# One written order for the recurrence's preparation and its loop: fillers placed by each iteration's room, modulation parts apart

## The chip, the core and the metric

The kernel runs on one core of one Trainium2 chip. The core has a matrix engine (TensorE, PE in the profile; PEld are its weight loads), a vector engine (VectorE, DVE), an engine for activation functions (ScalarE, ACT), a general engine (GpSimd, POOL) and SyncE (SP), which here only issues DMA transfers. Each engine works through its own instructions in the order in which they stand; a semaphore makes one wait for another. The metric is the time of one execution in microseconds (us), lower is better; the figure given for a kernel is the median of its runs.

## The reference

One layer of a diffusion backbone over 256 latent and 256 context tokens, width 2048, in fp32. The parts that matter here:

```python
m_lat = jnp.split((silu(c) @ w_mod + b_mod), 6)            # modulation rows
h  = modulate(rmsnorm(x, norm1_g), m_lat[0], m_lat[1])
P  = h @ w_in                                              # dense projection
b_r = rwkv_branch(P)          # two directions, 16 heads, state carried over time
b_c = conformer_branch(P)     # ends in u @ w_conv_out
m  = (sigmoid(P_gate_r) * b_r + sigmoid(P_gate_c) * b_c) @ w_o
x  = x + m_lat[2] * m
x  = x + m_lat[5] * ec_moe(modulate(rmsnorm(x, norm2_g), m_lat[3], m_lat[4]))
out = rmsnorm(x, final_g)
```

The recurrence inside `rwkv_branch` is `S_t = S_{t-1} (diag(w_t) - kk_t^T (kk_t * a_t)) + v_t^T k_t`, `y_t = S_t r_t`. The modulation rows 2 to 5 are first needed after the recurrence, and so are the two gates of 2048 columns each.

## The kernel before

The program runs in stages: norms, the first modulation rows and the projections that feed the recurrence (to about 540 us), the recurrence with its preparation (540 to 1295 us), two output projections (to 1470 us), and sixteen experts, whose weights stream in (to the end).

**The recurrence.** There are 16 units, a pair of heads in one direction each (`units`, 8 pairs x 2). A unit is a Python generator, `rwkv_dir`, which is cut by `yield` into named steps: D0 to D6 (loads `km`, `kn`, `rm`, `lw`, `vm`; decay and gates by a small matmul with `lwh` and `lwl`, L664 and L665; scans; `KB` and `VK`), C0 to C5 (transposes L761, scores L750), A0 to A7 (inverse of a triangular block: L845, L852, L867, L877, L887) and B0 to Z6 and B2 (L893, then L914, which is the first matmul of the chain over time, then seven links L932 with an ACT copy `Z` in between, then the outputs L938 and L942). `run(i, last)` drives unit i until it yields `last`, so a step is the code ahead of its `yield`. Units of the second direction go on through the group norm, G0 to G3 (L982, L987, L993).

**The loop.** Iteration i runs the B steps of unit i, the A steps of unit i+1, the C steps of unit i+2 and the D steps of unit i+3. The table `PLAN` gives each step a number on a scale of 36 for one iteration; everything is sorted by that number and written out. Inside `tc.manual_schedule` PE and DVE keep the written order; ACT, POOL and SP are ordered by the scheduler from its own timeline.

**The fillers.** Between the steps stand pieces of dense work that the recurrence doesn't need. A *gate part* (`gate_part`) is half of a block of four 128x128 weights: six matmuls L234 to L236 on a bank `big`. Its weights come as `wraw` (DMA), are split into `whi` (ACT, L159) and `wlo` (POOL, L230), three buffers each. There are 320 parts; the last 16 are held back until after the loop, the first 12 are issued ahead of the preparation at low priority (`early`), and 292 are in the loop. A *modulation part* (`mod_steps`, `part`) is four matmuls of 512 columns (L284; two records each in the trace) on 1 MB of `w_mod`, which is loaded into `wm`. There is one `wm` buffer. Four parts make a row; after the fourth ACT copies the sum back into the `wm` buffer, and `finish` turns the row into a column (L301) and adds the bias on DVE. `finish` is put on the list `later` and runs when the next modulation part is due, that is, directly ahead of the first part of the next row. Eight rows are in the loop, one in every second iteration (the even ones).

`spread` gives each of the 16 iterations the same total weight of fillers (a gate part counts 0.5 and a modulation part 0.5), and the fillers of an iteration stand at even distances on the scale.

**The preparation.** Before the loop, unit 0 has to come through D, C and A, unit 1 through D and C, and unit 2 through D. These six calls of `run` stand ahead of `manual_schedule`, and the scheduler orders all engines there.

Of the kernel before, what the change touches and what calls it, by code (L numbers as in the profile page):

```python
# [32 lines left out]
HOLD = 2  # L33
# [33 lines left out]
MN = 4  # L67
# [4 lines left out]
REL = [[0], [2], [4]]  # L72
LOWP = 1500
F0, F1 = 0.5, 36.0
PLAN = [(0, 0, "B0"), (4.5, 0, "B1"), (6.5, 0, "Z0"), (8.5, 0, "Z1"), (10.5, 0, "Z2"), (12.5, 0, "Z3"), (14.5, 0, "Z4"), (16.5, 0, "Z5"), (18.5, 0, "Z6"),
# [4 lines left out]
MODS = [8]  # L80
# [61 lines left out]
def kernel(  # L142
# [450 lines left out]
    modf = [f for _, f in mids]  # L593

    def weave2(a, b):
        nc_ = 16 - MODS[0]
        m = len(b) // nc_ if nc_ else 1
        at = lambda i: (i // m + 0.1 + MSP * (i % m + 0.5) / m) / nc_
        t = sorted([((i + 0.5) / len(a), 0, i) for i in range(len(a))] + [(at(i), 1, i) for i in range(len(b))])
        return [(a, b)[n][i] for _, n, i in t]  # L600

    def spread(l):
        n, c, o = sum(w for w, _ in l), 0, [[] for _ in range(16)]
        for w, f in l:
            o[int((c + 0.5 * w) * 16 / n)].append(f)
            c += w
        return o

    fills = spread(weave2(gates, mids))
    pend, acc = [], [0.0, 1.0]  # L610

    def tick(c):
        if not PUMP:
            return
        acc[0] += c
        while pend and acc[0] >= acc[1]:
            acc[0] -= acc[1]
            flush(1)

    def flush(n):  # L620
        with tc.high_priority(offset=-LOWP):
            for f in pend[:n]:
                while later and f in modf:
                    later.pop(0)()
                f()
            del pend[:n]

    rw_stack = ExitStack()
    rw = rw_stack.enter_context(tc.tile_pool(name="rw", bufs=1))
    BUF = dict(VK=1, KB=1, a2=7, rm=2, bon=3, RB=3, WCk=3, t4=2, VU=3, KBt=3, t2=3, NT8=2, t1=5, tx=2, c2=3,   # L630
               ys=3, Pv=1, km=1, kn=1, gw=2, bonr=1, tmp=2)
# [8 lines left out]
    def rwkv_dir(p, d, bonr, bon, INP):  # L640
# [223 lines left out]
        for cp, h, c, q in each():  # L864
            a, b, i = 64 * q + e, 64 * q + o, 2 * cp + h
            tick(0.03)
            PE.matmul(pq[b:b + 32, i, 0:32], AT[a:a + 32, c, h, o:o + 32], T2[a:a + 32, i], start=True, stop=True)  # L867
# [6 lines left out]
        for cp, h, c, q in each():  # L874
            a, b, i = 64 * q + e, 64 * q + o, 2 * cp + h
            tick(0.03)
            PE.matmul(pq[a:a + 32, i, 0:32], Q[b:b + 32, i], TT[b:b + 32, i], start=True, stop=True)  # L877
# [7 lines left out]
        for cp, h, c, q in each():  # L885
            tick(0.07)
            mark["pv"] = PE.matmul(pv[hs(q), cp, h], AT[hs(1 - q), c, h], VU[hs(1 - q), c, h], start=True, stop=True)  # L887
# [142 lines left out]
    def fill(f):  # L1030
        while later and f in modf:
            later.pop(0)()
        f()
# [390 lines left out]
```

## Time and profile before

| what | time |
|---|---|
| runs shown | 2429.71 and 2433.34 us, median 2431.53 us |
| the profiled execution | 2426.3 us, its span 2424.5 us |
| last projection matmul of the stage ahead | ends at 540.4 us |
| L914 of unit 0 (the chain over time begins) | 612.3 us |
| L993 of the last unit (the last matmul of the recurrence) | ends at 1295.3 us |
| first matmul of the experts | 1480.4 us |

A *window* is below the time from one unit's first L914 to the next one's; it is an iteration's length as PE sees it, shifted a little against the scale (L914 stands at 4.5 of 36). A row of the windows view gives a stretch (start:end in us), its length, for each engine its busy time and number of records, then the granted PE clock (1.00 is full speed), the busy share of the DMA engines and GB/s. A row of the timeline gives start, duration, engine, line, operation, tiles, shapes and count, and in brackets the idle time ahead of it and what ended it.

### The profile page before, as it was taken

To read this page: it belongs to the slowest core of one execution; us is meant where nothing else is said; L and a number is where in the kernel's file an instruction comes from. 1 tells how busy PE (TensorE), PEld (TensorE's weight loads), DVE (VectorE), ACT (ScalarE), POOL (GpSimd) and SP (SyncE) were. 2 spreads that over 40 slices of the span, in tenths; PEclk is the share of its full clock that TensorE was granted. 3 is DMA by queue.
4 is the path that set the end of the run, shared out by engine and by line. 5 is a ranking of instruction groups with operands and counts; after the bars stand their busy time and mean duration, and the time that the engine had idled before them with its cause. 6 is when DMAs were issued, how large, how long until landed. Compare 5 with 4: busy or idle time off the path is not lost.

```text
span 2424.5 us, 49050 instructions
## 1 busy us (share of the span) xinstructions
PE 2002.5 (83%) x20778; PEld 1413.1 (58%) x20778; DVE 920.7 (38%) x1821; ACT 777.5 (32%) x1540; POOL 675.5 (28%) x706
## 2 busy tenths in 40 slices
PE   7999999995889789888978997877777777777765
PEld 3787888884768668667768994433333333333332
DVE  2348989425545445445322542212111111111112
ACT  3255344634556446446444551000000000000002
POOL 1343334335555456445435741000000000000002
PEclk9999999995989889889989998989888899898887
DMA  9958767662343443444345887999999999999995
GB/s 383 347 176 292 244 202 238 215 215 84 129 149 108 138 145 114 146 150 116 113 152 168 285 303 320 427 428 427 428 427 427 428 428 427 427 427 428 428 417 222
DMA packets 147228, 674.43 MB, mean 278 GB/s; under 512 B 17600, under 2 KB 38208, under 8 KB 109888
## 3 DMA queue, kind: packets, MB, share of 16 engines
q1 hardware_dynamic: 129488, 459.68, 52.2%
q10 hardware_dynamic: 17520, 211.61, 20.7%
q8 instruction: 163, 2.67, 0.5%
q14 instruction: 57, 0.47, 0.1%
HBM read 649.41 MB, written 21.82 MB: 277 GB/s over the span
## 4 chain that ended last, share of the span: by engine, by line
DMA 28%; PE 18%; ACT 2%; DVE 1%; issue 1%; POOL 1%; SPq 1%; ACTq 0%; DVEq 0%; POOLq 0%
DMA wx<-in_w_dn 17%; DMA wx<-in_w_gu 9%; PE rw L1266 3%; PE p L1335 2%; PE gn L1335 2%; PE rw L234 1%; PE rw L1295 1%; PE rw L236 1%; PE rw L235 1%; PE big L1303 1%; ACT ye L159 1%; DMA wm<-in_w_mod 1%; PE big L234 1%; PE big L235 0%; PE big L236 0%
## 5 line engine op out<-in xcount | busy, mean ns | idle before, releaser
L230 POOL TENSOR_TENSOR wlo<-wraw,whi 128x512 fp32r<-128x512 f32 x292 | 400.1, 1373 | 513.2 <-ACT whi L159 455.6
L1303 PE MATMUL big<-wx,xse 128*32 128x512 f32 x2048 | 299.7, 719 | 153.9 <-DMA wx<-in_w_gu 152.0
L159 ACT ACTIVATE whi<-wraw 128x512 fp32r<-128x512 f32 x428 | 264.0, 628 | 332.5 <-DMA wraw<-in_w_in 102.4
L234 PE MATMUL big<-hh,whi 128*128 128x256 f32 x912 | 282.3, 310 | 2.7 <-ACT whi L159 2.7
L1303 PEld LDWEIGHTS big<-wx,xse 128*32 128x32 f32 x2048 | 63.7, 122 | 356.0 <-issue 179.9
L1279 POOL TENSOR_TENSOR r<-r 128x256 f32<-128x256 f32 x11 | 8.0, 731 | 921.1 <-ACT r L1275 920.5
L236 PE MATMUL big<-hh,wlo 128*128 128x256 f32 x912 | 261.1, 287 | 0.6 <-POOL wlo L230 0.6
L235 PE MATMUL big<-hl,whi 128*128 128x256 f32 x912 | 261.4, 287 | 0.0
L234 PEld LDWEIGHTS big<-hh,whi 128*128 128x128 f32 x912 | 176.3, 193 | 29.4 <-issue 18.6
L1316 ACT ACTIVATE th<-big 128x256 f32<-128x256 f32 x16 | 6.1, 384 | 576.2 <-PE big L1303 465.8
L235 PEld LDWEIGHTS big<-hl,whi 128*128 128x128 f32 x912 | 177.2, 194 | 5.0 <-issue 4.2
L236 PEld LDWEIGHTS big<-hh,wlo 128*128 128x128 f32 x912 | 176.4, 194 | 3.7 <-POOL wlo L230 2.0
L1270 DVE SCALAR_TENSOR_TENSOR x<-rw,modT,x 128x256 f32<-128x256 f32 x256 | 111.3, 479 | 134.6 <-PE rw L1266 134.4
L1317 DVE SCALAR_TENSOR_TENSOR th<-th,big 128x256 f32<-128x256 f32 x16 | 6.7, 421 | 404.7 <-ACT th L1316 404.7
L1266 PE MATMUL rw<-oT,ye 128*128 128x256 f32 x512 | 135.0, 408 | 29.1 <-ACT ye L159 28.3
L230 DVE TENSOR_TENSOR wlo<-wraw,whi 128x512 fp32r<-128x512 f32 x136 | 119.4, 883 | 90.3 <-ACT whi L159 76.5
L236 PE MATMUL rw<-hh,wlo 128*128 128x256 f32 x512 | 147.5, 289 | 4.6 <-POOL wlo L230 4.6
L479 DVE SCALAR_TENSOR_TENSOR cv<-up,hcw,cv 128x256 f32<-128x256 f32 x240 | 146.4, 611 | 9.2 <-POOL lsum L485 1.5
L234 PE MATMUL rw<-hh,whi 128*128 128x256 f32 x512 | 148.1, 291 | 0.6 <-ACT whi L159 0.4
L235 PE MATMUL rw<-hl,whi 128*128 128x256 f32 x512 | 147.0, 289 | 0.1
L1266 PEld LDWEIGHTS rw<-oT,ye 128*128 128x128 f32 x512 | 97.0, 200 | 79.1 <-ACT ye L159 63.4
L1295 PEld LDWEIGHTS rw<-oh,xk 128*128 128x128 f32 x1024 | 123.0, 194 | 31.1 <-issue 28.3
(354 smaller groups left out, 3794.9 us busy)
## 6 DMA issues: line engine op xcount, KB each, us to landing
wx<-in_w_gu ACTq DMA_DIRECT2D x66, 2048.0 KB, 39.1
wx<-in_w_gu SPq DMA_DIRECT2D x61, 2048.0 KB, 39.1
wm<-in_w_mod SPq DMA_DIRECT2D x96, 1024.0 KB, 6.8
wraw<-in_w_in SPq DMA_DIRECT2D x300, 256.0 KB, 3.6
wx<-in_w_dn ACTq DMA_DIRECT2D x32, 2048.0 KB, 38.6
wx<-in_w_dn SPq DMA_DIRECT2D x31, 2048.0 KB, 38.2
wraw<-in_w_o SPq DMA_DIRECT2D x64, 256.0 KB, 5.4
wraw<-in_w_co SPq DMA_DIRECT2D x32, 256.0 KB, 2.7
```

Source lines behind the costliest of these rows:

```text
L159: return ACT.activation(o, i, AF.Copy, scale=scale)
L230: (POOL if LO[0] < LO[1] else DVE).tensor_tensor(lo, raw, hi, op=OP.subtract)
L234: PE.matmul(o, hi, xh, start=start, stop=False, skip_group_check=True)
L235: PE.matmul(o, hi, xl, start=False, stop=False, skip_group_check=True)
L236: PE.matmul(o, lo, xh, start=False, stop=stop, skip_group_check=True)
L479: DVE.scalar_tensor_tensor(o, up[:, :, j:j + 64], hcw[:, i * KC + j:i * KC + j + 1], o, op0=OP.mult, op1=OP.add)
L1266: PE.matmul(pq[:, 256 * q:256 * q + 256], y[:, 128 * q:128 * q + 128], oT, start=True, stop=True)
L1270: DVE.scalar_tensor_tensor(x, pq[:, 256 * q:256 * q + 256], modT[:, 5, k + q, 0:1], x, op0=OP.mult, op1=OP.add)
L1279: POOL.tensor_tensor(r4[:, 0], r4[:, 0], sq, op=OP.add)
L1295: PE.matmul(pxs[:, k], xk[:, s, k], oh[:, s, e], start=(s == 0), stop=(s == 1))
L1303: PE.matmul(pg[32 * j:32 * j + 32, :], xs[:, k, :], w[:, a:a + 512], start=(k == 0), stop=(k == KD - 1))
L1335: PE.matmul(pd[32 * j:32 * j + 32, u], aT[:, 128 * b + 32 * j:128 * b + 32 * j + 32], w[:, 2 * j + b, u], start=(b == 0), stop=(b == 1))
```

## The change

1. The preparation is written into the same sorted list as the loop, with numbers from -47 to 0 for its steps (table `PRO`), and all of it stands inside `manual_schedule`: PE and DVE now keep the written order there too.
2. There is no `early` group. 30 gate parts stand at even distances in the preparation, 274 in the loop, and the 16 held ones as before.
3. An iteration's number of gate parts follows its room: `load` gives the PE time of an iteration without gate parts (22.9, less 1.3, 7.2 and 6.8 where units run out, 5.3 more with a modulation row), and the rest of the mean is filled at 0.73 for a part. That makes 11 parts in the even iterations from 0 to 12, 19 in the odd ones from 1 to 11, then 20, 23 and 40 in the last three (before: about 16 in even and 20 in odd ones).
4. The four parts of a modulation row stand at 3, 9, 15 and 21 of 36, and its `finish` at 23.5 in the same iteration.
5. The tile `rm` gets four buffers in place of two.

```diff
-F0, F1 = 0.5, 36.0
+TI = 36.0
+PRO = [(-44, 0, "D1"), (-42.5, 0, "D2"), (-39.5, 0, "D3"), (-36.5, 0, "D4"), (-34, 0, "D5"), (-33, 0, "D6"),
...
+FPRO = 30
+FT = 0.73
+MODT = (3, 9, 15, 21, 23.5)
...
-    na, nb = 6 * NZ * EARLY, len(parts) - 4 * NZ * HOLD
-    early, held = parts[:na], parts[nb:]
-    gates = [(1 / NZ, f) for f in parts[na:nb]]
-    mids = [(MW, f) for m in mods[MODS[0]:] for f in mod_steps(*m, mid, MN, MB, later, MP2)]
...
-    fills = spread(weave2(gates, mids))
...
+    nb = len(parts) - 4 * NZ * HOLD
+    gates, held = parts[:nb], parts[nb:]
...
-    BUF = dict(VK=1, KB=1, a2=7, rm=2, bon=3, RB=3, ...
+    BUF = dict(VK=1, KB=1, a2=7, rm=4, bon=3, RB=3, ...
...
-    with tc.high_priority(offset=-LOWP):
-        for f in early:
-            f()
-    run(0, "D6")
-    run(0, "C5")
-    run(1, "D6")
-    run(0, "A7")
-    run(1, "C5")
-    run(2, "D6")
...
+    nu = len(units)
+    todo = [(t, run, (o, s)) for t, o, s in PRO]
+    todo += [(TI * i + t, run, (i + o, s)) for i in range(nu) for t, o, s in PLAN]
+    todo += [(TI * (i + 1) - 0.01, reload_y, (slice(a, a + 2),)) for i in range(nu - len(REL), nu) for a in REL[i - nu + len(REL)]]
+    load = [22.9 - (1.3 if i + 3 >= nu else 0) - (7.2 if i + 2 >= nu else 0) - (6.8 if i + 1 >= nu else 0) for i in range(nu)]
+    for c, m in enumerate(mods[MODS[0]:]):
+        i = 2 * c
+        load[i] += 5.3
+        fs = mod_steps(*m, mid, MN, MB, later, MP2) + [lambda: later.pop(0)()]
+        todo += [(TI * i + t, f, ()) for t, f in zip(MODT, fs)]
+    room = (sum(load) + FT * (len(gates) - FPRO)) / nu
+    slots = [(-TI - 10 + (TI + 10) * (j + 0.5) / FPRO) for j in range(FPRO)]
+    want = 0.0
+    for i in range(nu):
+        want += (room - load[i]) / FT
+        n = int(want + 0.5) - (len(slots) - FPRO)
+        slots += [TI * (i + (j + 0.5) / n) for j in range(n)]
+    todo += [(t, f, ()) for t, f in zip(slots, gates)]
     with tc.manual_schedule(engines=MANUAL(nc)):
-        for i in range(len(units)):
-            n = len(fills[i])
-            todo = [(t, run, (i + o, s)) for t, o, s in PLAN] + [(F0 + F1 * (j + 0.5) / n, fill, (f,)) for j, f in enumerate(fills[i])]
-            for t, f, a in sorted(todo, key=lambda x: x[0]):
-                f(*a)
...
+        for t, f, a in sorted(todo, key=lambda x: x[0]):
+            f(*a)
```

**Where it shows in the order.** Line numbers of the changed kernel are 10 higher up to the table and 26 lower in `rwkv_dir`: L234 is L244, L284 is L294, L301 is L311, L664 is L638.

First place, PE, iteration 2, a modulation row (`wm`, `slp`) among the links of the chain (`Z`, `PT`). Before, with the second three matmuls of each gate part left out, from the turn of the old row to the second part of the new one:

```order
L664 MATMUL p_7916<-zs_1398,lwh 128x512
L665 MATMUL p_7916<-zs_1398,lwl 128x512
L301 MATMUL p_7925<-C,wm 128x1 x4
L284 MATMUL big<-wm,slp 32x512 x4
L932 MATMUL gn<-Z,PT 64x64 x2
L845 MATMUL sb<-T,X 32x32 x32
L750 MATMUL rw<-VK,KB 128x64 x8
L234 MATMUL big<-hh_92,whi 128x256
L235 MATMUL big<-hl_93,whi 128x256
L236 MATMUL big<-hh_92,wlo 128x256
L284 MATMUL big<-wm,slp 32x512 x4
```

PE, the same iteration in the changed kernel, from just ahead of the row's fourth part to its turn:

```order
L901 MATMUL gn<-Z,PT 64x64 x2
L826 MATMUL sb<-Q,TT 32x32 x32
L907 MATMUL gn<-KM,VU 64x64 x8
L911 MATMUL gn<-RB,Z 64x64 x8
L294 MATMUL big<-wm,slp 32x512 x4
L244 MATMUL big<-hh_92,whi 128x256
L245 MATMUL big<-hl_93,whi 128x256
L246 MATMUL big<-hh_92,wlo 128x256
L840 MATMUL sb<-T_8255,AT 32x32 x16
L311 MATMUL p_8331<-C,wm 128x1 x4
```

The turn moved from directly ahead of the next row's first part to directly behind its own fourth part, almost two iterations earlier.

Second place, SP, the loads of that row. Before, from the first part's load to the fourth's (`wm`), among the loads of later units (`km`, `vm`, `kn`, `rm`):

```order
L276 DMA wm<-in_w_mod 128x2048
L649 DMA km<-kd 128x512
L276 DMA wm<-in_w_mod 128x2048
L713 DMA vm<-vd 128x512
L651 DMA kn<-kd 128x512
L653 DMA rm<-rd 128x256
L276 DMA wm<-in_w_mod 128x2048
L227 DMA wraw<-in_w_in 128x512 x2
L276 DMA wm<-in_w_mod 128x2048
```

SP in the changed kernel, from the second part's load to that of the next row's first part:

```order
L286 DMA wm<-in_w_mod 128x2048
L237 DMA wraw<-in_w_in 128x512
L286 DMA wm<-in_w_mod 128x2048
L629 DMA lw<-in_lora 128x256
L623 DMA km<-kd 128x512
L627 DMA rm<-rd 128x256
L687 DMA vm<-vd 128x512
L237 DMA wraw<-in_w_in 128x512
L625 DMA kn<-kd 128x512
L286 DMA wm<-in_w_mod 128x2048
L237 DMA wraw<-in_w_in 128x512
L286 DMA wm<-in_w_mod 128x2048
```

The first part's load moved an iteration ahead (the last row), and of the others it is now the fourth's that stands behind `kn`, where it was the third's.

Third place, PE in the preparation, from the decay matmuls of a unit to the scores of unit 0 (`VK`, `KB`). Before:

```order
L664 MATMUL p_5909<-zs_1397,lwh 128x512
L665 MATMUL p_5909<-zs_1397,lwl 128x512
L664 MATMUL p_5919<-zs_1397,lwh 128x512
L665 MATMUL p_5919<-zs_1397,lwl 128x512
L761 MATMUL rw<-C,VK 128x128 x8
L750 MATMUL rw<-VK,KB 128x128 x8
L750 MATMUL rw<-VK,KB 128x64 x2
L725 MATMUL p_5946<-rk,bonr 128x256
```

In the changed kernel, with repeated rows of gate parts left out (six parts stand between the first L638 shown, of unit 1, and the scores of unit 0, L724):

```order
L638 MATMUL p_5886<-zs_1398,lwh 128x512
L639 MATMUL p_5886<-zs_1398,lwl 128x512
L244 MATMUL big<-hh_92,whi 128x256
L245 MATMUL big<-hl_93,whi 128x256
L246 MATMUL big<-hh_92,wlo 128x256
L638 MATMUL p_5915<-zs_1398,lwh 128x512
L639 MATMUL p_5915<-zs_1398,lwl 128x512
L699 MATMUL p_5960<-rk,bonr 128x256
L735 MATMUL rw<-C,VK 128x128 x4
L724 MATMUL rw<-VK,KB 128x128 x8
```

The scores of unit 0 moved behind the decay matmuls of unit 1 and six gate parts.

More of the change, by code (lines that the diff above doesn't have):

```diff
@@ L588 @@
     parts = [lambda n=n, z=z: gate_part(n, z) for n in range(len(srcs)) for z in range(NZ)]
-    na, nb = 6 * NZ * EARLY, len(parts) - 4 * NZ * HOLD
-    early, held = parts[:na], parts[nb:]
-    gates = [(1 / NZ, f) for f in parts[na:nb]]
-    mids = [(MW, f) for m in mods[MODS[0]:] for f in mod_steps(*m, mid, MN, MB, later, MP2)]
[L593 to L607, printed above, removed]
-    fills = spread(weave2(gates, mids))
[L610 to L620, printed above, removed]
-        with tc.high_priority(offset=-LOWP):
-            for f in pend[:n]:
-                while later and f in modf:
-                    later.pop(0)()
-                f()
-            del pend[:n]
+    nb = len(parts) - 4 * NZ * HOLD
+    gates, held = parts[:nb], parts[nb:]
     rw_stack = ExitStack()
     rw = rw_stack.enter_context(tc.tile_pool(name="rw", bufs=1))
-    BUF = dict(VK=1, KB=1, a2=7, rm=2, bon=3, RB=3, WCk=3, t4=2, VU=3, KBt=3, t2=3, NT8=2, t1=5, tx=2, c2=3,
+    BUF = dict(VK=1, KB=1, a2=7, rm=4, bon=3, RB=3, WCk=3, t4=2, VU=3, KBt=3, t2=3, NT8=2, t1=5, tx=2, c2=3,
                ys=3, Pv=1, km=1, kn=1, gw=2, bonr=1, tmp=2)
@@ L865, in rwkv_dir @@
             a, b, i = 64 * q + e, 64 * q + o, 2 * cp + h
-            tick(0.03)
             PE.matmul(pq[b:b + 32, i, 0:32], AT[a:a + 32, c, h, o:o + 32], T2[a:a + 32, i], start=True, stop=True)
@@ L875, in rwkv_dir @@
             a, b, i = 64 * q + e, 64 * q + o, 2 * cp + h
-            tick(0.03)
             PE.matmul(pq[a:a + 32, i, 0:32], Q[b:b + 32, i], TT[b:b + 32, i], start=True, stop=True)
@@ L885, in rwkv_dir @@
         for cp, h, c, q in each():
-            tick(0.07)
             mark["pv"] = PE.matmul(pv[hs(q), cp, h], AT[hs(1 - q), c, h], VU[hs(1 - q), c, h], start=True, stop=True)
@@ L891, in rwkv_dir @@
         for cp, h, c, q in each():
-            tick(0.12)
             PE.matmul(ku[cp // 2][hs(q), cp % 2, h], TT[hs(q), cp, h], VU[hs(q), c:9 + cp:8 + cp - c, h], start=True, stop=True)
@@ L906, in rwkv_dir @@
                 hh_ = h if b == 0 else 1 - h
-                tick(0.1)
                 lhs, o = KN[hs(q), cp, hh_], PP[j][hs(hh_)]
@@ L1018, in run @@
             pass
-    with tc.high_priority(offset=-LOWP):
-        for f in early:
-            f()
-    run(0, "D6")
-    run(0, "C5")
-    run(1, "D6")
-    run(0, "A7")
-    run(1, "C5")
-    run(2, "D6")
[L1030 to L1033, printed above, removed]
-    with tc.manual_schedule(engines=MANUAL(nc)):
-        for i in range(len(units)):
-            n = len(fills[i])
-            todo = [(t, run, (i + o, s)) for t, o, s in PLAN] + [(F0 + F1 * (j + 0.5) / n, fill, (f,)) for j, f in enumerate(fills[i])]
-            for t, f, a in sorted(todo, key=lambda x: x[0]):
-                f(*a)
-            if i >= 16 - len(REL):
-                for a in REL[i - 16 + len(REL)]:
-                    reload_y(slice(a, a + 2))
+    nu = len(units)
[16 more added lines that the diff above has]
+    todo += [(t, f, ()) for t, f in zip(slots, gates)]
+    assert len(slots) == len(gates)
+    with tc.manual_schedule(engines=MANUAL(nc)):
+        for t, f, a in sorted(todo, key=lambda x: x[0]):
+            f(*a)
     with tc.high_priority(offset=-LOWP):
```

6 rows, old and new, of the table PRO are left out of this document.

## Prediction

> **What bounds the kernel now.** First the cores view and the slices of the page: one slice is 60.6 us.
>
> ```profile
> core 0: 2424.5 us, clock 0.899
> ```
>
> ```profile
> PEclk9999999995989889889989998989888899898887
> DMA  9958767662343443444345887999999999999995
> ```
>
> From slice 26 on (1515 us, the experts) the DMA engines are full, so that stage keeps its length and only starts earlier. In slices 10 to 22 (the recurrence) they are a fifth to a half busy, and the granted clock falls below full speed again and again. So I cut the recurrence by the windows view:
>
> ```profile
> 540.40:612.25 71.85, 42.59 (x526) 34.46 (x527) 38.52 (x65) 33.14 (x64) 37.16 (x47) 0.57 0.32 98
> 612.25:1295.30 683.05, 587.78 (x10397) 482.83 (x10397) 308.32 (x642) 368.35 (x785) 343.67 (x337) 0.90 0.43 133
> 657.15:693.24 36.09, 35.14 (x677) 30.94 (x676) 20.97 (x43) 25.38 (x55) 25.60 (x24) 1.00 0.39 114
> 693.24:748.30 55.06, 41.53 (x693) 32.58 (x692) 21.51 (x49) 23.90 (x51) 21.46 (x24) 0.85 0.45 142
> 1224.30:1275.50 51.20, 39.89 (x647) 31.24 (x646) 12.83 (x30) 16.96 (x40) 14.06 (x11) 0.77 0.52 171
> 1275.54:1295.32 19.78, 19.43 (x219) 17.34 (x219) 2.52 (x7) 10.43 (x22) 10.43 (x9) 1.00 0.42 121
> ```
>
> The preparation takes 71.85 us at clock 0.57, the sixteen windows 683.05. An odd window (657.15) has PE busy for 35.14 of 36.09 us at full clock: it is bound by PE. An even one (693.24) lasts 55.06, with 13.5 us idle and clock 0.85. The sums of the eight even windows, then of the seven odd ones up to 13:
>
> ```profile
> sum 412.56, PE 324.94 PEld 250.73 DVE 161.14 ACT 180.35 POOL 165.65; mean PE 40.62 PEld 31.34 DVE 20.14 ACT 22.54 POOL 20.71
> ```
>
> ```profile
> sum 250.69, PE 243.39 PEld 214.78 DVE 144.68 ACT 177.57 POOL 167.61; mean PE 34.77 PEld 30.68 DVE 20.67 ACT 25.37 POOL 23.94
> ```
>
> So 51.6 against 35.8 us, for a row of modulation parts. The waits of PE from 605 to 1300 us say why:
>
> ```profile
> PE big L284 <- DMA wm<-in_w_mod: 81.6, 25, 7.0
> PE gn L993 <- ACT ysq L988: 3.3, 5, 1.1
> ```
>
> Nearly all idle time of the loop is the wait of modulation parts for their weights. One row of iteration 2, PE and then SP:
>
> ```profile
> 701.64 1.05 PE L301 MATMUL p<-C,wm 128*128 128x1 f32 x8 [0.85 <-ACT ta L684]
> 708.38 1.94 PE L284 MATMUL big<-wm,slp 128*32 128x512 f32 x8 [5.69 <-DMA wm<-in_w_mod]
> ...
> 724.74 1.07 PE L284 MATMUL big<-wm,slp 128*32 128x512 f32 x8 [2.66 <-DMA wm<-in_w_mod]
> ...
> 732.66 1.07 PE L284 MATMUL big<-wm,slp 128*32 128x512 f32 x8 [4.04 <-DMA wm<-in_w_mod]
> ```
>
> ```profile
> 702.73 0.33 SPq L276 DMA_DIRECT2D wm<-in_w_mod  x1
> 703.81 0.33 SPq L649 DMA_DIRECT2D km<-kd  x1
> 710.38 0.33 SPq L276 DMA_DIRECT2D wm<-in_w_mod  x1
> 714.37 0.33 SPq L713 DMA_DIRECT2D vm<-vd  x1
> 717.71 0.33 SPq L651 DMA_DIRECT2D kn<-kd  x1
> 718.35 0.32 SPq L653 DMA_DIRECT2D rm<-rd  x1
> 718.77 1.44 SPq L276 DMA_DIRECT2D wm<-in_w_mod  x1
> ```
>
> Three causes are visible. The first load goes out only behind the turn L301, which still reads the single `wm` buffer, so the first part waits 5.69 us. The third load stands behind `kn`, which POOL's write of `VK` has to release. And the parts stand too close: a load takes 5.7 to 6.0 us from issue to its part (702.73 to 708.38, 718.77 to 724.74). The waits also cool the clock:
>
> ```profile
> 709.00:716.00 7.00, 7.00 (x106) 4.86 (x102) 2.33 (x4) 2.23 (x5) 0.28 (x1) 0.50 0.52 167
> 717.00:733.00 16.00, 9.30 (x278) 7.05 (x278) 4.67 (x7) 4.23 (x10) 5.66 (x8) 1.00 0.59 190
> 734.00:737.00 3.00, 3.00 (x39) 2.94 (x34) 0.00 (x0) 2.49 (x7) 0.00 (x0) 0.50 0.02 5
> ```
>
> Behind the waits of 5.69 and 4.04 us the clock is 0.50; behind the one of 2.66 us it stays 1.00.
>
> **The change part by part.**
>
> *A gate part's price.* The rows of `big` matmuls alone: in an odd window (120 of them, 20 parts; the last, and the sum of seven), and in a stretch where four parts stand in a row.
>
> ```profile
> 1190.10:1224.30 34.20, 18.32 (x121) 15.26 (x120) 0.00 (x0) 0.75 (x2) 1.00 0.33 91
> sum 250.69, PE 131.16 PEld 108.67 DVE 4.15 ACT 5.25; mean PE 18.74 PEld 15.52 DVE 0.59 ACT 0.75
> ```
>
> ```profile
> 649.82:652.70 2.88, 2.88 (x26) 2.80 (x24) 0.42 (x1) 0.36 (x1) 1.00 0.42 130
> ```
>
> 18.74 / 20 = 0.94 us standing alone, 2.88 / 4 = 0.72 in a row. I take 0.88, nearer the first, as most parts still stand alone.
>
> *Even windows 0 to 10.* From an odd window: 36.1 less its idle 0.95, less 9 parts (20 to 11) x 0.88 = 7.9, plus four modulation parts x 1.07 and the turn 1.05: 32.6 us. Waits: the first part's load is issued an iteration ahead, so its 5.69 us go. Parts stand 6 of 36 apart, 6.3 us in a window of 38; the next one needs 1.07 + 0.1 + 5.8 = 7.0 us from the start of the one before. That leaves 0.7 us each at the second and third part (bounds 0 and 2). The fourth part's load is now the one behind `kn`. In an odd window POOL starts the `VK` write 14.4 us after the start (657.15):
>
> ```profile
> 671.56 1.18 POOL L717 TENSOR_TENSOR VK<-kn,Wp 128x512 f32<-128x512 f32 x1
> ```
>
> It ends at 15.6; the load follows 0.4 to 1.1 us later and lands 5.8 us after, at 22.2. The part's place is 16.5 of 36 behind L914, at 17.3 to 18.7 once the earlier waits are counted, so it waits 3.5 us (bounds 1.5, if `VK` comes sooner with nothing cold ahead of it, and 6). While PE stands there, the chain's next step, the inverse of the next unit and all gate parts stand too. A wait of 3.5 us lies between the 2.66 that left the clock alone and the 4.04 that halved it; I add 1 us. Sum: 32.6 + 1.4 + 3.5 + 1 = 38.5, six times 231.
>
> *Windows 12 and 14* have no `kn` in the queue any more: 32.6 + 1.5 = 34 for 12. Window 14: 51.20 less 11.3 idle is 39.9; at clock 0.77 nearly half of it ran at half speed, worth some 6 us; six more parts cost 5.3: 39 us.
>
> *Odd windows 1 to 11*: one part fewer, 36.1 - 0.9 = 35.2, six times 211. *13*: unchanged, 34.2. *15*: 19.78 + 23 parts x 0.8 = 38.5 (a few of them move behind L993).
>
> Sum: 231 + 34 + 39 + 211 + 34 + 38.5 = 587.5, against 683.05: **-95.5 us**.
>
> *Preparation.* 18 more parts run in it, in PE time that was idle (42.59 busy of 71.85, and that at clock 0.57); they are already counted as missing from the loop. Its length is set by unit 0's dependencies. Before, the scores waited for DVE and that for POOL:
>
> ```profile
> 559.72 1.74 DVE L705 SCALAR_TENSOR_TENSOR Wy<-di,Wy 128x520 f32<-128x520 f32 x1 [3.08 <-POOL di L702]
> ```
>
> ```profile
> 557.67 1.97 PE L761 MATMUL rw<-C,VK 128*128 128x128 f32 x8 [7.21 <-POOL VK L717]
> 563.77 2.82 PE L750 MATMUL rw<-VK,KB 64*128 64x128 f32 x20 [4.14 <-DVE KB L709]
> ```
>
> POOL's order is the scheduler's still, with `di` behind the `VK` writes as before and `lwl` of unit 1 ahead of it. So PE, now bound to the written order, waits for that `lwl` until about 558 and then has six parts ahead of the scores, at first at half clock (1.4 us each): scores about 6 us later than 563.77. Later the scans of unit 2 no longer cut into unit 0's inverse on DVE, PE is warm, and the steps up to L914 come 8 us faster. Net -2 us, bounds -12 and +10.
>
> *The turn* (eight records of L301, a 128x4 DVE addition) only moves; ACT's copy ahead of it has a gate part and L840 for cover, about 1.6 us against 0.6; without them PE would wait about 0.8 us a row. *`rm`'s buffers* take loads out of the queue's blocked stretch: nothing. Behind L993 the held parts and what follows stay as they are (bounds -3 and +3).
>
> Total: 2426.3 - 95.5 - 2 = **2329 us** for the profiled execution. The median of the runs lies 5 us above that execution, so I say 2331.
>
> **The rivals.**
>
> *1. The fourth part stays as late as the worst waits now and goes cold.* With 6 us and a clock at 0.50 behind it (3 us), an even window is 43, six times 4.5 more: 2358. For it: SP's order has `kn` ahead of that load in six of the eight rows. Against: the parts ahead no longer wait, so `VK` comes as in an odd window. The Trainium skill, "TensorE: Matmul & The Clock Gate", section "HAM oscillation — how this bites in real kernels", says that a wait crossing one activity window of about 3.4 us halves the clock. The trace agrees (4.04 did, 2.66 did not), and by that rule each of the six waits would go cold, some 2 us more each, 2343. Chance 0.15.
>
> *2. PE stalls in the preparation.* In a fixed order one late `lwl` or `wlo` holds everything; if each of unit 1's two decay steps costs 7 us like the 7.21 above, it is +15: 2346. For it: POOL is busy 37.16 of 71.85 there with the scheduler's order. Chance 0.1.
>
> *3. The turn frees nothing*, because the scheduler's queue brings the first load late anyway: 5.7 us stay in seven rows, 2370. Against: that load stands right behind the fourth in SP's order, an iteration ahead. Chance 0.05.
>
> *4. Slower: the gate parts starve.* Their `wraw` loads share SP's queue with `kn`, `km` and `vm`; three buffers are six parts, about 11 us of cover in an odd window. If SP is blocked longer than that, PE waits for the excess in each iteration. To lose the gain the block has to reach 11 + 6 = 17 us in all sixteen; at 21 us the kernel takes 2490. Against it stand these rows of the page, in which 912 matmuls of each kind waited 3.3 us in all:
>
> ```profile
> L234 PE MATMUL big<-hh,whi 128*128 128x256 f32 x912 | 282.3, 310 | 2.7 <-ACT whi L159 2.7
> ...
> L236 PE MATMUL big<-hh,wlo 128*128 128x256 f32 x912 | 261.1, 287 | 0.6 <-POOL wlo L230 0.6
> ```
>
> Chance 0.02; a half of it, within 2% of now, 0.03.
>
> **How the numbers follow.** The forecast has 0.65, rivals 1 to 4 the rest. Low end: no waits at the second and third part, 1.5 at the fourth, no cold clock, is 4.4 x 6 = 26 us less, with 10 less in the preparation 2295; as both are unlikely together, 2304. High end: rival 1 with a slow preparation, 2366. All but rivals 3 and 4 lie in it. 2% of 2431.5 is 49 us, about what a measurement of this kernel can tell from no change: 2383 and below is faster, 0.95; within 0.03; slower 0.02.
>
> **What would show it.** Right: even windows of 36 to 41 us with clock near 1.00, odd ones near 35; the wait of modulation parts down from 81.6 to about 30 us, none at a row's first part, most at the fourth; L914 of unit 0 near 610 us; the last window near 38. Wrong: even windows above 43, waits of gate parts for `wlo` or `whi`, L914 of unit 0 after 625, or an odd window that no longer has PE busy, which would mean that the recurrence's own chain had taken the wait's place.

## The result, and the profile after

| | before | changed |
|---|---|---|
| time, median of two runs | 2431.53 us | 2365.25 us (2364.24 to 2366.26) |
| the profiled execution | 2426.3 us | 2366.26 us (span 2364.5) |
| projections: last step of the key norm (L429, now L439) | 524.26 | 529.02 |
| from there to unit 0's L914, now L883 | 87.99 | 93.70 |
| the sixteen windows | 683.05 | 602.28 |
| end of the windows to the first matmul on expert weights (L1303, now L1270) | 189.1 | 196.8 |
| experts to the end | 940.1 | 942.7 |

The ratio is 0.9727 with a 95% interval of 0.9686 to 0.9769: faster by 2.3 to 3.1%. The forecast was 2331 with a range of 2304 to 2366: the sign and the range hold, but the median lies 0.75 us inside the range's upper edge and the profiled execution just outside it. In six more runs (label d0 below) the changed kernel's median was 2354.71 and the ratio 0.971 [0.9682, 0.9737].

The windows view of the changed kernel, with the same columns as before (length, busy time of PE, PEld, DVE, ACT and POOL, granted clock, DMA share, GB/s): the loop, an odd window, window 12, window 14, window 15, and the stretch up to the first expert.

```profile
622.71:1224.99 602.28, 564.64 (x10277) 468.20 (x10277) 306.29 (x639) 359.37 (x773) 331.97 (x326) 0.94 0.46 146
662.50:699.10 36.60, 35.06 (x673) 29.85 (x672) 22.02 (x42) 25.67 (x55) 24.51 (x24) 1.00 0.37 112
1081.20:1115.20 34.00, 31.70 (x657) 25.38 (x656) 19.39 (x48) 21.04 (x46) 16.96 (x17) 1.00 0.55 182
1151.40:1194.40 43.00, 39.01 (x679) 31.87 (x678) 10.79 (x26) 18.27 (x43) 17.50 (x14) 0.92 0.59 195
1194.40:1224.99 30.59, 30.54 (x313) 28.37 (x313) 2.91 (x7) 15.62 (x32) 21.03 (x17) 1.00 0.54 158
1224.99:1421.80 196.81, 173.47 (x1364) 165.27 (x1363) 85.16 (x140) 88.72 (x168) 104.92 (x97) 0.91 0.76 262
```

The mean clock of the loop rose from 0.90 to 0.94. The clock records here hold only 1.0 and 0.5, so 0.94 means that about (1 - 0.94) x 2 = 12% of 602 us, some 72 us, still ran at half clock. The sums of the even windows 0 to 10, and then of the odd windows 1 to 11:

```profile
sum 234.19, PE 214.88 PEld 170.96 DVE 121.83 ACT 128.51 POOL 112.81; mean PE 35.81 PEld 28.49 DVE 20.30 ACT 21.42 POOL 18.80
sum 224.30, PE 213.63 PEld 181.56 DVE 135.79 ACT 153.04 POOL 146.93; mean PE 35.60 PEld 30.26 DVE 22.63 ACT 25.51 POOL 24.49
```

That is 39.0 us for an even window and 37.4 for an odd one. The waits of PE from 605 to 1225 us (in all, times, longest):

```profile
PE big L294 <- DMA wm<-in_w_mod: 16.3, 7, 3.6
PE gn L951 <- DVE ys L944: 4.7, 6, 1.9
PE sb L826 <- issue: 3.4, 2, 2.6
PE sb L819 <- DVE T L828: 3.3, 3, 1.1
PE gn L962 <- ACT ysq L957: 2.7, 7, 1.3
```

The wait of modulation parts fell from 81.6 to 16.3 us. What is left sits at one place. The parts and the turn of iteration 2, PE and then SP's queue; its third part ran at 711.91 without a wait:

```profile
697.53 1.06 PE L294 MATMUL big<-wm,slp 128*32 128x512 f32 x8
705.32 1.06 PE L294 MATMUL big<-wm,slp 128*32 128x512 f32 x8
...
721.07 1.93 PE L294 MATMUL big<-wm,slp 128*32 128x512 f32 x8 [2.38 <-DMA wm<-in_w_mod]
725.03 1.05 PE L311 MATMUL p<-C,wm 128*128 128x1 f32 x8
```

```profile
712.51 0.33 SPq L237 DMA_DIRECT2D wraw<-in_w_in  x1
714.58 0.32 SPq L625 DMA_DIRECT2D kn<-kd  x1
715.35 1.22 SPq L286 DMA_DIRECT2D wm<-in_w_mod  x1
```

The first three parts find their weights there. The fourth part's load leaves right behind `kn` at 715.35 and its part starts 5.7 us later, at 721.07, 22.0 us after the window's start at 699.1. The forecast had put that landing at 22.2. In five of the six even windows from 0 to 10 the fourth part waits 2.4 to 3.6 us, 14.8 us together, and each of these waits has a fall of the clock during it or within 0.8 us of its end. The same place in the windows view:

```profile
718.00:724.25 6.25, 3.87 (x34) 2.07 (x30) 2.35 (x5) 1.77 (x4) 0.72 (x2) 0.73 0.48 186
...
727.50:731.00 3.50, 3.50 (x41) 3.38 (x40) 0.00 (x0) 2.16 (x5) 2.46 (x3) 0.52 0.69 274
```

A wait of 2.38 us was enough: the clock fell to half during it, at 720.80, and once more at 727.63, where PE's records show no idle time ahead of it; that second fall stays unexplained. Before the change a wait of 2.66 us had left the clock at 1.00; the section on the hardware shows why.

### The profile page after: what moved, and what is told of

Read it like the earlier page. It is cut to its first block, busy times and chain, and to the rows that moved or that the text cites. A ratio compares the mean times of both kernels' runs of the same rounds, so it can differ in the third digit from the quotient of the medians.

```text
span 2364.5 us, 49070 instructions
## 1 busy us (share of the span) xinstructions
PE 1995.1 (84%) x20778; PEld 1410.6 (60%) x20778; DVE 924.5 (39%) x1821; ACT 774.4 (33%) x1540; POOL 673.3 (28%) x706
## 3 DMA queue, kind: packets, MB, share of 16 engines
q8 instruction: 163, 2.67, 0.5%
## 4 chain that ended last, share of the span: by engine, by line
DMA 33%; PE 32%; DVE 3%; POOL 3%; issue 2%; ACT 2%; SPq 0%; ACTq 0%; DVEq 0%; POOLq 0%
DMA wx<-in_w_gu 17%; DMA wx<-in_w_dn 13%; PE big L244 3%; PE big L246 2%; PE big L245 2%; DMA wm<-in_w_mod 2%; PE rw L1233 2%; PE rw L246 2%; PE rw L244 2%; PE rw L245 2%; PE big L1270 2%; PE p L1302 1%; PE big L294 1%; PE rw L1262 1%; PE rw L863 1%
## 5 line engine op out<-in xcount | busy, mean ns | idle before, releaser
L1270 PE MATMUL big<-wx,xse 128*32 128x512 f32 x2048 | 300.1, 720 | 157.2 <-DMA wx<-in_w_gu 154.9
L244 PE MATMUL big<-hh,whi 128*128 128x256 f32 x912 | 288.7, 317 | 3.4 <-ACT whi L169 3.4
L1270 PEld LDWEIGHTS big<-wx,xse 128*32 128x32 f32 x2048 | 63.2, 121 | 356.7 <-DMA wx<-in_w_gu 177.0
L246 PE MATMUL big<-hh,wlo 128*128 128x256 f32 x912 | 266.2, 292 | 5.7 <-POOL wlo L240 5.6
L244 PEld LDWEIGHTS big<-hh,whi 128*128 128x128 f32 x912 | 180.8, 198 | 39.9 <-issue 27.9
L240 DVE TENSOR_TENSOR wlo<-wraw,whi 128x512 fp32r<-128x512 f32 x136 | 114.6, 847 | 100.8 <-ACT whi L169 86.6
L244 PE MATMUL rw<-hh,whi 128*128 128x256 f32 x512 | 147.4, 289 | 3.0 <-ACT whi L169 3.0
L1262 PEld LDWEIGHTS rw<-oh,xk 128*128 128x128 f32 x1024 | 124.3, 195 | 35.5 <-issue 28.3
## 6 DMA issues: line engine op xcount, KB each, us to landing
wx<-in_w_dn SPq DMA_DIRECT2D x31, 2048.0 KB, 38.5
```

Source lines behind the costliest of these rows:

```text
L240: (POOL if LO[0] < LO[1] else DVE).tensor_tensor(lo, raw, hi, op=OP.subtract)
L244: PE.matmul(o, hi, xh, start=start, stop=False, skip_group_check=True)
L246: PE.matmul(o, lo, xh, start=False, stop=stop, skip_group_check=True)
L1262: PE.matmul(pxs[:, k], xk[:, s, k], oh[:, s, e], start=(s == 0), stop=(s == 1))
L1270: PE.matmul(pg[32 * j:32 * j + 32, :], xs[:, k, :], w[:, a:a + 512], start=(k == 0), stop=(k == KD - 1))
```

## The experiments

Eleven runs, in four groups; each group shares runs of the kernel before (medians 2428.94, 2427.70, 2427.61 and 2422.68). "Preparation" is the time from the last key-norm step of the projections to unit 0's L883 (L914 in kernels made from the one before), "loop" the sixteen windows, both of the one profiled execution. The start of the preparation isn't comparable between executions. The same program up to that point ends the projections 8.4 us apart, in the profile of before and in that of b1:

```profile
524.26 0.27 PE L429 MATMUL p<-C,rn 128*16 128x128 f32 x1
```

```profile
532.66 0.27 PE L429 MATMUL p<-C,rn 128*16 128x128 f32 x1
```

| label | median us | ratio, 95% interval | preparation | loop | clock in it | waits for `wm` |
|---|---|---|---|---|---|---|
| d0_after_again | 2354.71 | 0.971 [0.9682, 0.9737] | 91.7 | 611.1 | 0.93 | 18.2 |
| e1_prep_scheduler | 2356.86 | 0.971 [0.968, 0.974] | 94.8 | 590.2 | 0.96 | 16.0 |
| e4_prep_12_parts | 2346.11 | 0.9665 [0.9639, 0.9692] | 86.1 | 598.5 | 0.97 | 14.8 |
| e3_part4_late | 2328.21 | 0.9592 [0.9563, 0.962] | 92.2 | 577.0 | 0.98 | 0.2 |
| e2_turn_late | 2407.16 | 0.9906 [0.9881, 0.9931] | 92.8 | 646.0 | 0.92 | 56.5 |
| b1_turn_only | 2391.90 | 0.9854 [0.9818, 0.9891] | 88.2 | 645.1 | 0.92 | 51.1 |
| c1_late4_12_parts | 2332.07 | 0.9599 [0.9561, 0.9637] | 85.7 | 579.1 | 0.99 | 5.9 |
| c2_late4_split_dve | 2327.87 | 0.9588 [0.9553, 0.9623] | 87.1 | 571.0 | 0.99 | 2.1 |
| c3_late4_norm | 2320.09 | 0.9558 [0.952, 0.9596] | 91.9 | 564.2 | 1.00 | 3.0 |
| d2_norm_equal | 2347.55 | 0.9678 [0.965, 0.9707] | 92.6 | 592.6 | 0.97 | 2.6 |
| d1_all | 2315.16 | 0.9537 [0.951, 0.9564] | 86.6 | 559.3 | 1.00 | 2.2 |

**The mark.** No edit.

> The changed kernel as it is, timed in more runs, as the mark for the other runs. Expected 2355 to 2370. L883 of unit 0 lies 92 to 95 us behind the last L439 of the projections, and the cold stretches of the loop differ from those of the first profile, since a wait of 2 to 3.5 us cools the clock only in some windows.

Six runs, 2351.68 to 2368.78; the profiled one was the slowest of them. The median and the preparation of 91.7 us both lie 0.3 us below what was expected.

**The fourth part later.**

```diff
-MODT = (3, 9, 15, 21, 23.5)
+MODT = (3, 9, 15, 28.5, 31)
```

> The changed kernel with the fourth modulation part of a row moved from 21 to 28.5 and the turn from 23.5 to 31. Theory C (the even windows' rest of 39.1 against about 34 us is one wait of 2.4 to 3.6 us for the fourth part's weights, and the clock of 0.50 that follows it for 3.5 to 13.8 us): no wait at that part, clock of the even windows 0.97 or more, windows of 33.5 to 35.5, total 2330 to 2342. Rival D (another wait takes its place: kn, VK and the next unit's scores, or a turn that now comes late for the next row's load): even windows stay above 37.5, total 2355 or more.

2328.21 us, theory C, 2 us below its range. The loop, window 2 (the counterpart of the one at 699.1 above), and the sum of the even windows 0 to 10, 34.4 us each:

```profile
623.30:1200.30 577.00, 547.16 (x10277) 451.93 (x10277) 298.50 (x639) 358.81 (x773) 332.45 (x326) 0.98 0.47 152
694.50:728.80 34.30, 32.21 (x655) 25.37 (x654) 19.92 (x47) 20.89 (x48) 18.96 (x21) 1.00 0.57 198
...
sum 206.10, PE 194.18 PEld 152.33 DVE 116.78 ACT 128.10 POOL 112.72; mean PE 32.36 PEld 25.39 DVE 19.46 ACT 21.35 POOL 18.79
```

The same matmuls stand in the loop (x10277 in both), and PE's busy time fell from 564.64 to 547.16: these 17.5 us were matmuls at half clock. The waits that went are 16.1 us. The loop is 25.3 us shorter: 17.5 of busy and 7.8 of idle time, since half of the time waited comes back in small waits for other things (5.0 us in all at the turn, for the copy ahead of it). So the rest of the even windows was the fourth part's wait, and more of it was the clock behind that wait than the wait. What cold stretches are left in this loop stand behind other waits: two named "issue" (1.87 and 2.58 us), one for `ys` (1.04) and one for `ysq` (2.66).

**The turn.** First the changed kernel with the turn left to the next row, then the kernel before with nothing but the early turn.

```diff
-        fs = mod_steps(*m, mid, MN, MB, later, MP2) + [lambda: later.pop(0)()]
+        fs = mod_steps(*m, mid, MN, MB, later, MP2)
+        if c:
+            fs[0] = lambda f=fs[0]: (later.pop(0)(), f())
```

> The changed kernel with each row's turn left until the next row's first part, as before the change. Theory E (turning at once is what lets the first part's load go out early): a wait of 5.5 to 6 us at the first part of seven rows, each followed by a clock of 0.50 for some 7 us, 7 x 9 = 63 us more: about 2428, as slow as before the change. Rival F (the spacing of 6 and the room did the work): within 20 us of the changed kernel, 2365 to 2385.

2407.16, between the two theories. The waits grew by 40 us: in each of seven odd windows, where a row's first part stands, PE waits 4.9 to 6.9 us for `wm`, and the odd windows 1 to 11 took 45.2 us in place of 37.4. Over the loop a late turn cost 6.2 us (43.7 more in seven rows), not the 9 expected: PE's busy time in the loop is only 5 us above that of the changed kernel (569.68 and 564.64), so the clock added little.

```diff
-    mids = [(MW, f) for m in mods[MODS[0]:] for f in mod_steps(*m, mid, MN, MB, later, MP2)]
+    mids = [(w, f) for m in mods[MODS[0]:] for w, f in [(MW, f) for f in mod_steps(*m, mid, MN, MB, later, MP2)] + [(0, lambda: None)]]
...
-        at = lambda i: (i // m + 0.1 + MSP * (i % m + 0.5) / m) / nc_
+        at = lambda i: (i // m + 0.1 + MSP * (i % m + 0.5) / 4) / nc_
```

> The kernel before the change, with one thing of the change alone: each row's turn follows its fourth part at once. Order, spacing and gate parts are left as they were. Theory E (the late turn held back the first load): the wait of some 5.5 us at a row's first part goes in seven rows, with part of the cold clock behind it, 7 x 5.5 to 7 x 9 us less: 2365 to 2392. Rival G (the parts stand too close for the load cycle of about 7 us, so the time given back at the first part is waited at the others): the waits of modulation parts stay above 65 of the 81.6 us, total above 2410.

The added entry does nothing itself: ahead of it the pending turn is issued, as ahead of each part. (It takes one of the even distances of its iteration, so the other pieces there move a little.) 2391.90, theory E's slow end; the waits fell from 81.6 to 51.1 us:

```profile
PE big L284 <- DMA wm<-in_w_mod: 51.1, 23, 5.6
```

So the turn alone is worth 36 us (2427.70 to 2391.90), everything else alone 22 (2428.94 to 2407.16), 58 us in sum, and the changed kernel, with both, gained 66 to 73. Rival 3 of the prediction falls.

**The preparation: order or load.** First the order given back to the scheduler with the same 30 parts, then the written order with 12.

```diff
-    todo = [(t, run, (o, s)) for t, o, s in PRO]
+    with tc.high_priority(offset=-LOWP):
+        for f in gates[:FPRO]:
+            f()
+    run(0, "D6")
+    run(0, "C5")
+    run(1, "D6")
+    run(0, "A7")
+    run(1, "C5")
+    run(2, "D6")
+    todo = []
```

> The changed kernel, with its preparation given back to the scheduler: the same 30 gate parts, now as low-priority filler. The loop is the same. Theory A (the written order is what lengthened the preparation from 71.9 to 82.3 us: PE stands behind operands that are not there yet): L883 of unit 0, at 622.7 in the changed kernel, comes at 605 to 612, and the kernel takes about 2353. Theory B (the 18 further gate parts did it in any order, because their splits on POOL slow the inverse on DVE and delay VK): L883 stays at 618 or later, total 2360 to 2370.

```diff
-FPRO = 30
+FPRO = 12
```

> The changed kernel with 12 gate parts in the written preparation in place of 30 (FPRO); the 18 others are shared out over the loop. Theory A (order): L883 stays within 3 us of 622.7, the loop grows by 18 x 0.95 = 17 us, total about 2382. Theory B (POOL's splits): L883 comes at 612 or earlier, with the steps of the inverse on DVE (L797, L805) back from up to 1.2 us to about 0.2 us each; with 17 us more in the loop the total is about 2371.

Read from the end of the projections, e1 needs 94.8 us, as long as the changed kernel; the written order isn't what costs. Its total, 2356.86, lies between the two theories, so the stage decides. With 12 parts it is 86.1. The expected time of L883 itself (612 or earlier; it was 620.5) was missed, since the projections ended 10 us later in that execution than in the profile of before. Missed too was the inverse on DVE: its steps did not come back to 0.2 us each (below). The total of e4, 2346, is below what either theory gave: its loop has 18 more parts and is yet 4 us shorter than in the first profile of the changed kernel, with a clock of 0.97 for 0.94. That this was the clock and not the parts is what the same edit on top of e3 says:

> The version with the fourth part at 28.5 (2328.2 us median, cold clock rare), and besides it 12 gate parts in the preparation in place of 30. With the clock near full in the loop, the price of the parts is read without it. Theory B (30 parts cost the preparation some 7 us through POOL, while each part costs the loop 0.95): preparation 7 us shorter from the last step of the projections to L883, loop 17 us longer, total 2333 to 2342. Rival H (the gain of 19 us that 12 parts gave with the fourth part at 21 was the parts themselves, not a clock that happened to stay up): total 2305 to 2320.

2332.07 against 2328.21 in another group, ratios 0.9599 and 0.9592: no difference. Preparation 6.6 us shorter, PE's busy time in the loop 10.6 us more (557.72 and 547.16, the clock 0.99 and 0.98). The loop was 2.1 us longer in these two profiles (579.1 and 577.0) and not the expected 17: c1's profile had less half clock in it, 13.7 us in place of 23.9, and 8.4 us less idle time of PE; neither was asked for by the edit. Rival H falls.

What 30 parts do to the preparation is seen on DVE. Unit 0's inverse consists of small steps, each waiting for the one before. In the changed kernel, DVE and then POOL beside it:

```profile
587.19 0.76 DVE L797 TENSOR_TENSOR tmp<-N 128x24 f32<-128x24 f32 x1
587.98 1.22 DVE L805 TENSOR_TENSOR N<-N,tmp 128x24 f32<-128x24 f32 x1
589.23 0.30 DVE L797 TENSOR_TENSOR tmp<-N 128x40 f32<-128x40 f32 x1
589.57 1.22 DVE L805 TENSOR_TENSOR N<-N,tmp 128x40 f32<-128x40 f32 x1
```

```profile
587.84 1.29 POOL L240 TENSOR_TENSOR wlo<-wraw,whi 128x512 fp32r<-128x512 f32 x1
...
589.45 1.28 POOL L240 TENSOR_TENSOR wlo<-wraw,whi 128x512 fp32r<-128x512 f32 x1
```

The same steps before the change:

```profile
574.91 0.20 DVE L831 TENSOR_TENSOR N<-N,tmp 128x24 f32<-128x24 f32 x1
...
575.38 0.20 DVE L831 TENSOR_TENSOR N<-N,tmp 128x40 f32<-128x40 f32 x1
```

A step of 0.20 us takes 1.22 and ends when POOL's `wlo` does (587.98 + 1.22 = 589.20; 587.84 + 1.29 = 589.13). The twelve steps sum to 2.9 us before and 8.6 after; with 12 parts they still take 6.1 (e4) and 6.4 (c1), so it matters beside what the splits fall, and not only how many they are. So the next run takes the splits off POOL and leaves the parts and the order (on top of e3):

```diff
+    def split_on(a):
+        LO[1:] = [a, 1]
+
+    todo = [(-60, split_on, (0,)), (-0.5, split_on, (1,))]
-    todo = [(t, run, (o, s)) for t, o, s in PRO]
+    todo += [(t, run, (o, s)) for t, o, s in PRO]
```

> The version with the fourth part at 28.5, with the splits of the weights (L240) of the preparation's gate parts on DVE in place of POOL; same 30 parts, same written order. Theory B (POOL's splits hold up VK and slow the small DVE steps of unit 0's inverse): the twelve steps L797 and L805 take 5 us or less in sum in place of 8.6, and L883 comes 4 us or more sooner, total about 2322. Rival I (DVE, which runs in written order, now waits for whi in front of the chain): L883 the same or later, total 2328 to 2340.

The steps sum to 5.6 us, above the 5 expected; other POOL work (`kp`, `rk`, `ta`) still stands beside some. The preparation takes 87.1 in place of 92.2 us, no longer than before the change with 12 parts; d1 below, with the same edit, has 86.6, and the six profiles with 30 parts in this order and their splits on POOL have 91.7 to 93.7. Of the 5 us, 1.8 lie ahead of the chain of steps, 1.8 in it (10.4 to 8.6 us from its first start to its last end) and 1.4 behind it. Among DVE's rows a split now costs 0.68 us, with POOL idle beside this one; two splits stand inside the chain:

```profile
590.17 0.68 DVE L240 TENSOR_TENSOR wlo<-wraw,whi 128x512 fp32r<-128x512 f32 x1
```

The total, 2327.87, lies between the two expectations and isn't measurably below that of e3: 5 us are lost in a spread of 10 us from run to run. The shorter preparation is shown by the profiles, a gain in total time is not.

**What was left in the windows.** The group norm's steps later:

```diff
-        (21, 0, "B2"), (23, 0, "G0"), (25, 0, "G1"), (28.5, 0, "G2"), (33, 0, "G3"),
+        (21, 0, "B2"), (23, 0, "G0"), (26.6, 0, "G1"), (30.5, 0, "G2"), (34.5, 0, "G3"),
```

> The version with the fourth part at 28.5, with the three steps of the group norm moved from 25, 28.5 and 33 to 26.6, 30.5 and 34.5. In the odd windows PE waits 1.0 us for ys at L951 and up to 0.5 for ysq at L962. If these waits are on PE's path: odd windows 1 us shorter, windows 12 and 13 without the cold stretch behind ysq, total 2312 to 2322. If the steps only trade places: within 5 us of 2328.

2320.09, as expected, though its interval still overlaps that of e3. The odd windows 1 to 11 went from 37.2 to 36.3 us, and the loop's clock reads 1.00:

```profile
622.44:1186.60 564.16, 537.52 (x10283) 444.35 (x10283) 300.63 (x639) 359.84 (x774) 330.22 (x327) 1.00 0.49 156
```

The windows 12 and 13, 41.0 and 39.0 us in e3, took 34.1 and 36.1. In window 13 the cold stretch of e3 began in the wait of 2.66 us for `ysq`, and no wait for `ysq` is now longer than 1.0; in window 12 it began in a wait named "issue", so those 7 us of the 12.8 by which the loop is shorter can't be put down to the edit.

On this version, the room taken away, so that every iteration gets about 15 gate parts:

```diff
-        load[i] += 5.3
```

> The version with the fourth part at 28.5 and the later steps of the group norm (2320.1 us, no cold stretch in its loop), without the allowance of 5.3 us for a row of modulation parts in the count of gate parts: about 15 parts in each iteration in place of 11 and 19 by turns. Theory J (with the waits gone PE is busy through both kinds of window, so that a part costs the same 0.95 us wherever it stands): even windows 3.5 to 4 us longer, odd ones as much shorter, loop within 6 us of 564, total 2314 to 2328. Rival K (with 15 parts an odd window can't cover the recurrence's own chain, so that PE waits there and goes cold): odd windows no shorter than 34.5, total 2332 or more.

2347.55: rival K. The odd windows took 36.1 us, about what they took with 19 parts (36.3), the even ones 38.1 in place of 34.0. The waits of PE from 616 to 1190 us:

```profile
PE gn L962 <- ACT ysq L957: 9.4, 7, 1.6
PE sb L826 <- issue: 7.9, 3, 3.5
PE sb L819 <- DVE T L828: 5.9, 7, 1.0
PE sb L849 <- ACT Q L169: 5.6, 8, 1.3
```

With 15 parts an odd window has 3 us of idle time spread over `ysq`, `T` and `Q`: the recurrence's own chain needs some 36 us whatever is put between. But the four cold stretches came in the even windows, behind waits of 1.8 to 3.5 us named "issue"; so the mechanism of K holds for the odd windows, and its clock does not.

**All together.** The edits of c2 and c3, and the turn later still:

```diff
-MODT = (3, 9, 15, 28.5, 31)
+MODT = (3, 9, 15, 28.5, 33)
```

> The fourth part at 28.5, the later steps of the group norm, the preparation's splits on DVE, and the turn at 33 instead of 31 (the version with the later norm waits 0.7 us at the turn in seven windows). If the gains add: 2320 less 5 for the preparation less 5 for the turn, 2306 to 2314, no cold stretch in the loop, L883 some 87 us behind the last L439. If the turn at 33 makes the next row's first load late, or the splits disturb DVE: above 2318.

2315.16 (2306.96 to 2320.72), just above the expected 2306 to 2314; one cold stretch of 3.4 us is left in the loop, behind a wait named "issue". It is 4.6% faster than the kernel before and beats the changed one; that it beats c3 isn't settled, since their intervals overlap.

## Why the prediction was right, and where its sum was off

The sum stood at 2426.3 - 97.5 = 2328.8 for a profiled execution; the profile of the change has 2366.26, 37 us more. By the windows and stages below, that is 16 us in the pairs of windows, 6 in windows 12 to 14, nothing in window 15 and the tail together, 8 in the preparation, 5 in the projections and 3 in the experts.

That the time still fell into the range is in part luck. The upper edge was put at "rival 1 with a slow preparation, 2366", but by the prediction's own terms that is 2358 and 12 more, 2370; and what brought the time there, a cold clock and a slow preparation, was not in the forecast itself. The direction, the place of the gain (the waits of modulation parts) and the place of the rest (the fourth part) were not luck. Of the signs that it named, the even windows and the waits held; a clock near 1.00 in the even windows (0.83 to 0.95 in windows 0 to 10), L914 near 610 (L883 came at 622.7) and a last window near 38 us (30.6) did not.

- **The waits: right.** No wait at a row's first part, and the fourth behind `kn` with its landing 22 us into the window. The waits for `wm` came to 16.3 us, where "about 30" had been put; the second and third part waited for nothing in windows 0 to 10. e2 and b1 show that the early turn is what frees the first part.
- **The clock: the step that failed.** "I add 1 us", because 3.5 us "lies between the 2.66 that left the clock alone and the 4.04 that halved it". The five waits came out at 2.4 to 3.6 us, four of them shorter than the 3.5 assumed, and all five cooled. PE's busy time per even window was 35.8 us against 32.4 in e3 (its same six windows), so the clock cost 3.4 us and not 1. Rival 1 named the place and the cold clock; it took a wait twice as long, and its 2358 was nearer than the forecast. One number of one trace had been made into a threshold, while it is the place of a wait that decides with its length (below).
- **A gate part: mis-sized, but not a cause.** 0.88 us was taken, "as most parts still stand alone". The rows of `big` matmuls alone in the odd window at 662.5 give 18.15 us:

```profile
662.50:699.10 36.60, 18.15 (x116) 1.00 0.37 112
```

  Less one modulation part of 1.07 that is 17.1 / 18 = 0.95: in the written order all stand alone. The sum only took parts away, ten from a pair of windows, so with 0.95 the forecast would have been 0.7 us a pair lower, farther from the result.
- **One part in the wrong window.** The first part stands ahead of L883, at the end of the odd window before. The pair is what to compare: 38.5 + 35.2 = 73.7 forecast, 39.0 + 37.4 = 76.4 measured, six times 2.7 = 16 us. That the even window alone came out at 39.0 for 38.5 is luck: it has one part less, shorter waits and a dearer clock. Window 7 (40.6 us) also went cold, behind 1.94 us of waiting for `ys`.
- **Windows 12 to 14.** 12 took 34.0, as forecast. 13 took 36.3 for 34.2; it holds the first part of the last row. 14 took 43.0 for 39, at clock 0.92; it holds 50 of L244's matmuls, two to a gate part, where 34 of L234's stood before: eight parts more, and six had been counted.
- **The last window and the tail belong together.** 38.5 was forecast for window 15 and nothing after it. It took 30.6, with 65 of L244's matmuls, some 32 parts in place of 40: the others stand in window 14 and behind L962. The stretch to the experts took 7.7 us more, with half-clock stretches of 13.7 and 3.4 us at its start in place of one of 6.8.
- **The preparation: wrong in sign, inside its bounds.** "Net -2": it took 5.7 us more from the same point. The first half held: the scores come 3.9 us later and unit 0's inverse begins on DVE 7.8 us later (58.2 in place of 50.4 behind the key norm), where about 6 had been put. That "the steps up to L914 come 8 us faster" was the false step: from the inverse's first step on DVE they came 2 us faster (35.5 in place of 37.6). The part behind the inverse's last step on DVE gained 9.2 us, and the chain of twelve steps lost 7.1 of them (10.4 us from first start to last end in place of 3.3), 5.7 in the steps themselves, which wait for POOL; the prediction had put POOL's work beside that chain at nothing. c2 and d1 show POOL's splits as a part of it and e4 and c1 the number of parts; even so the steps don't come back to 2.9 us in any of them. Rival 2 blamed the fixed order; e1 shows that the scheduler's order is no better.
- **The projections** ended 4.8 us later. b1 has the same program up to there as the kernel before and ended another 3.6 us later, so nothing shows this to be an effect of the change.

## What to carry to other kernels

A load that stands on the queue behind another one that has to wait for data is late by that wait: place its consumer by the time at which it can land (here 22 us into the window). Here that, with the turn behind it, was worth some 26 us (2354.71 to 2328.21, medians of two groups). Where PE is warm, count an idle gap of 2 us as dear as its length and the cold clock together, and look for gaps with the clock row beside the waits. When filler is put into a stretch with idle PE time, count what the filler does on the other engines: the parts fitted on PE, but their splits on POOL ran beside a chain on DVE, whose steps took 8.6 us in place of 2.9 (6.1 with 12 parts).

## What the runs showed of the hardware

**The clock falls after shorter waits than one trace told, and not always.** In the loops of thirteen profiles (the eleven runs and the two first ones; waits that began at full clock) the clock was halved during a wait of PE or within 3.5 us of its end in 15 of 26 waits of 1.5 to 2 us, in 26 of 31 of 2 to 3 us, and in all 42 above 3 us. Cold stretches last 3.4, 6.8, 10.2 or 13.7 us (one 23.9), steps of about 3.4. The Trainium skill, "TensorE: Matmul & The Clock Gate", section "HAM oscillation — how this bites in real kernels", gives the rule as no idle gaps of more than about 3.4 us. These runs agree with the step and not with the limit.

What decides in most cases is how much idle time falls into one step. The clock records of each profile begin and end on one grid of 3.413 us, to within 5 ns. Of the grid's steps in these loops that began at full clock, the clock fell at the end of all 62 in which PE was idle for 1.8 us or more, of 30 of the 110 with 1.0 to 1.8 us, and of 5 of the 1923 with less. The wait of 2.66 us before the change lay across an edge of the grid, with about 1.3 us of idle time in the step on each side (first two rows); the one of 2.38 us after it lay with 2.1 us in one step, which had 2.3 us of idle time in all (third row):

```profile
719.99:723.41 3.42, 2.10 (x78) 1.72 (x78) 1.43 (x1) 2.02 (x5) 2.27 (x3) 1.00 0.81 278
723.41:726.82 3.41, 2.08 (x75) 1.20 (x76) 0.28 (x1) 0.00 (x0) 0.00 (x0) 1.00 0.70 214
```

```profile
717.39:720.80 3.41, 1.07 (x25) 0.86 (x24) 2.96 (x5) 1.17 (x3) 1.33 (x3) 1.00 0.88 324
```

So the two waits, of nearly the same length, differ by where they lay; this is read from the profiles, and no run moved a wait along the grid alone.

**A small DVE step waits for a whole POOL instruction.** Of the 192 steps of the inverse in the changed kernel's profile, 25 began while POOL ran a two-operand instruction, and their median is 1.22 us; for the other 167 it is 0.20. The Trainium skill, "SBUF — State Buffer", section "Who interferes with whom", says that a DVE instruction with two SBUF inputs and a GpSimd instruction that reads SBUF exclude each other for the whole instruction. The trace agrees, with 0.20 against 1.22 us.

**PE can run out of instructions.** The longest of the waits named "issue", in d2:

```profile
711.48 0.70 PE L826 MATMUL sb<-Q,TT 32*32 32x32 f32 x59
715.72 0.32 PE L826 MATMUL sb<-Q,TT 32*32 32x32 f32 x5 [3.54 <-issue]
```

PE stops between two of 64 equal small matmuls. The page of the changed kernel lists 20,778 matmuls and as many weight loads, and this queue:

```profile
q8 instruction: 163, 2.67, 0.5%
```

41,556 / 163 = 255 instructions for each packet of 16 KB (2.67 MB / 163). There are 22 such waits over 1.5 us in the loops of the changed kernel and the ten runs made from it (none in the kernel before and b1), and all end 2.2 to 2.5 us after a packet of this queue began. That the waits are for instructions follows from this agreement; no run took such a load away, so it is argued and not shown.
